# Row normalization on one core: a fixed transfer order on one queue, the last tile in halves, and a broadcast multiply

## The chip, the core and the metric

The kernel runs on one core of a Trainium2 chip. The metric is the device time of one execution in microseconds (us). Two engines compute here: VectorE (DVE in the profile, 190.8 us busy in the kernel before) and ScalarE (ACT, 56.7 us). SyncE (SP) issues the transfers between HBM and the on-chip memory (22 of them in the kernel before); the profile counts 16 DMA engines that carry them out.

In this text L3 is the load of tile 3 and S3 the store of tile 3; S7a and S7b are its first and second part where it is cut.

## The reference

```python
# x: float32 (32, 512, 1024)
sums = np.sum(np.abs(x), axis=-1, keepdims=True)
return (x / (sums + 1e-8)).astype(np.float32)
```

Each row of 1024 numbers is divided by the sum of its absolute values. 67.11 MB go in and 67.11 MB come out.

## The kernel before

The 16384 rows are cut into 8 tiles of 128 partitions x 16 rows. One tile is 8.39 MB; each partition's part of it is 64 KB, contiguous in HBM. Three tile buffers rotate.

```python
x_t = x_flat.rearrange("(n p r) d -> n p r d", p=P, r=R)       # R = 16
def process_chunk(x_tile, out_ap, r0, rN, mv):
    # ... cut: s = sum |x| per row, inv = 1 / s, both on VectorE; row = x_tile[:, r0 + r, :]
    for r in range(rN):
        if r < mv:
            nc.vector.tensor_scalar_mul(out=row, in0=row, scalar1=inv[:, r : r + 1])
        else:
            nc.scalar.activation(out=row, in_=row, func=Copy, scale=inv[:, r : r + 1])
    nc.sync.dma_start(out=out_ap[:, r0 : r0 + rN, :], in_=x_tile[:, r0 : r0 + rN, :])

for i in range(ntiles):
    nc.sync.dma_start(out=x_tile[:, :, :], in_=x_t[i, :, :, :])
    if i < ntiles - 2:
        process_chunk(x_tile, out_t[i], 0, R, 10)      # 10 rows on VectorE, 6 on ScalarE
    else:                                              # the last two tiles in quarters
        for c0 in range(0, R, 4):
            process_chunk(x_tile, out_t[i], c0, 4, 2)
```

The scheduler is free to order the instructions. On SyncE it made groups: L0-L2, S0-S2, L3-L5, S3-S5, L6, L7, then the eight quarter stores of tiles 6 and 7.

## Time and profile before

| | before |
|---|---|
| time, median of 3 | 318.28 us |
| span of the profile | 316.9 us |
| VectorE / ScalarE busy | 190.8 us (60%) / 56.7 us (18%) |
| DMA queue busy, share of 16 engines | 98.6% |
| bytes moved | 134.22 MB |

These lines are from the page of the kernel before: the busy time, the row of the 40 slices for DMA (each digit is the busy share in tenths), the queue with packets, MB and share, and the three costliest groups (line, engine, operation, shapes, count, then busy us, mean ns of one, and idle time before them with what ended it).

```profile
DVE 190.8 (60%) x104; ACT 56.7 (18%) x53; POOL 0.2 (0%) x4
DMA  9999999999999999999999999999999999999797
q1 hardware_dynamic: 3168, 134.22, 98.6%
L37 DVE TENSOR_REDUCE s<-x_tile 128x4 f32<-128x4096 f32 (+1 forms) x14 | 138.3, 9891 | 111.2 <-DMA x_tile<-in_x_dram 111.2
L54 ACT ACTIVATE x_tile<-x_tile,inv 128x1024 f32<-128x1024 f32 x52 | 55.4, 1137 | 223.9 <-DVE inv L45 223.9
L48 DVE TENSOR_SCALAR x_tile<-x_tile,inv 128x1024 f32<-128x1024 f32 x76 | 51.4, 748 | 0.3
```

The queue is full nearly everywhere, while VectorE waits 111 us for loads. The kernel is bound by its transfers. The one place where the queue is not full is near the end. The next lines are stretches of the same trace: from:to, length, busy us of VectorE, ScalarE and GpSimd, clock, DMA share, GB/s. (A packet seems to be booked where it starts, so a stretch near a packet's 2.4 us can swing, even above 1 (1.23 from 314 to 315 us of this trace).)

```profile
288.00:292.00 4.00, 4.00 (x3) 2.19 (x2) 0.00 (x0) 1.00 1.00 430
292.00:296.00 4.00, 4.00 (x6) 1.85 (x2) 0.00 (x0) 1.00 0.77 328
296.00:300.00 4.00, 4.00 (x4) 2.41 (x3) 0.00 (x0) 1.00 0.93 393
300.00:302.00 2.00, 1.97 (x5) 0.75 (x1) 0.00 (x0) 1.00 0.81 344
```

And these are two lines of SyncE's timeline there (start us, length, issue): the first quarter store of tile 7, and the other three.

```profile
294.09 0.33 SPq L60 DMA_DIRECT2D out_dram<-x_tile  x1
299.87 3.93 SPq L60 DMA_DIRECT2D out_dram<-x_tile  x3
```

VectorE is fully busy in these stretches. It is late with the second quarter of tile 7, and the queue runs short for a moment: that store was issued at 299.87 us, only 0.6 us before the store ahead of it had landed (300.43 us), and it landed 5.8 us after it, where the next two took 4.9 us each.

### The profile page before, as it was taken

The numbers are of one execution on the slowest core, as the hardware profiler recorded it, in microseconds if no ns is written. First come the engines' busy times: TensorE is split into PE (matmuls) and PEld (weight loads), VectorE is DVE, ScalarE is ACT, GpSimd is POOL, SyncE is SP. The second block draws the span as 40 slices with busy tenths as digits, with TensorE's granted clock in tenths as the row PEclk, the third lists the DMA queues.
The fourth block names the chain that finished last, engine by engine and source line by source line (L and its number), as shares of the span: only waits on it lengthen the run. The fifth ranks groups of instructions, "written<-read, shape, count | busy, mean of one in ns | idle before, by whom it ended". The sixth has DMA issues, their size and how long they took to land.

```text
span 316.9 us, 261 instructions
## 1 busy us (share of the span) xinstructions
DVE 190.8 (60%) x104; ACT 56.7 (18%) x53; POOL 0.2 (0%) x4
## 2 busy tenths in 40 slices
DVE  0019999999990000039999999980000069999910
ACT  0010080080080000000160070080000002522520
POOL 0000000000000000000000000000000000000000
DMA  9999999999999999999999999999999999999797
GB/s 397 397 397 513 414 397 397 397 438 488 397 397 505 422 397 397 521 405 397 480 447 397 397 489 438 397 430 480 414 397 480 438 405 422 399 431 432 335 430 331
DMA packets 3170, 134.24 MB, mean 424 GB/s; under 512 B 352, under 2 KB 352, under 8 KB 352
## 3 DMA queue, kind: packets, MB, share of 16 engines
q1 hardware_dynamic: 3168, 134.22, 98.6%
q14 instruction: 2, 0.02, 0.0%
HBM read 67.11 MB, written 67.11 MB: 424 GB/s over the span
## 4 chain that ended last, share of the span: by engine, by line
DVE 57%; DMA 35%; issue 4%; ACT 0%; ACTq 0%; SPq 0%; DVEq 0%
DVE s L37 41%; DMA x_tile<-in_x_dram 35%; DVE x_tile L48 15%; DVE inv L45 1%; ACT x_tile L54 0%; ACTq L99 0%; SPq L60 0%; DVEq L45 0%; DVEq L48 0%
## 5 line engine op out<-in xcount | busy, mean ns | idle before, releaser
L37 DVE TENSOR_REDUCE s<-x_tile 128x4 f32<-128x4096 f32 (+1 forms) x14 | 138.3, 9891 | 111.2 <-DMA x_tile<-in_x_dram 111.2
L54 ACT ACTIVATE x_tile<-x_tile,inv 128x1024 f32<-128x1024 f32 x52 | 55.4, 1137 | 223.9 <-DVE inv L45 223.9
L48 DVE TENSOR_SCALAR x_tile<-x_tile,inv 128x1024 f32<-128x1024 f32 x76 | 51.4, 748 | 0.3
L54 ACT ACT_TABLE_LOAD x1 | 1.3, 1283 | 22.8 <-DMA x_tile<-in_x_dram 22.8
L45 DVE RECIPROCAL inv<-s 128x4 f32<-128x4 f32 (+1 forms) x14 | 2.6, 200 | 0.4
L88 POOL MEMSET const-bfloat16-1.0<- 128x1 bf16 x1 | 0.1, 101 | 0.0
L88 POOL MEMSET const-uint8-127<- 128x1 uint8 x1 | 0.1, 101 | 0.0
L88 POOL MEMSET const-float32-0.0<- 128x1 f32 x1 | 0.1, 98 | 0.2 <-issue 0.2
L88 POOL MEMSET const-float32-1.0<- 128x1 f32 x1 | 0.1, 98 | 0.0
## 6 DMA issues: line engine op xcount, KB each, us to landing
out_dram<-x_tile SPq DMA_DIRECT2D x8, 2048.0 KB, 9.9
x_tile<-in_x_dram SPq DMA_DIRECT2D x8, 51.0
out_dram<-x_tile SPq DMA_DIRECT2D x6, 29.5
```

What stands on the lines that cost most here:

```text
L37: nc.vector.tensor_reduce(out=s[:, :], in_=x_tile[:, r0 : r0 + rN, :], axis=mybir.AxisListType.X, op=mybir.AluOpType.add, apply_absolute_v ...
L45: nc.vector.reciprocal(out=inv[:, :], in_=s[:, :])
L48: nc.vector.tensor_scalar_mul(out=x_tile[:, r0 + r, :], in0=x_tile[:, r0 + r, :], scalar1=inv[:, r : r + 1],)
L54: nc.scalar.activation(out=x_tile[:, r0 + r, :], in_=x_tile[:, r0 + r, :], func=mybir.ActivationFunctionType.Copy, scale=inv[:, r : r + 1],)
L88: nc = _bacc.Bacc("TRN2", target_bir_lowering=False, num_devices=1)
```

## The change

Its intent: keep one hardware queue always supplied, in an order written by hand (L0 L1 L2 S0 S1 L3 S2 L4 S3 L5 S4 L6 L7 S5 S6 S7); cut only the last tile, in halves; and replace the row-by-row VectorE multiplies by one multiply per tile.

```diff
+        nc.vector.tensor_scalar_add(out=s[:, :k], in0=s[:, :k], scalar1=EPS)
         ... reciprocal, as before ...
-        for r in range(rN):
-            if r < mv:
-                nc.vector.tensor_scalar_mul(out=row, in0=row, scalar1=inv[:, r : r + 1])
-            else: nc.scalar.activation(...)
+        nc.vector.tensor_mul(                                   # kv = k // 2
+            out=x_tile[:, r0 : r0 + kv, :],
+            in0=x_tile[:, r0 : r0 + kv, :],
+            in1=inv[:, :kv].unsqueeze(2).to_broadcast([P, kv, d]),
+        )
+        for r in range(kv, k): nc.scalar.activation(...)
     ... cut ...
+    plan = [("L", i) for i in range(BUFS)]
+    for i in range(ntiles):
+        plan.append(("S", i))
+        nxt = i + BUFS - 1
+        if BUFS <= nxt < ntiles:
+            plan.append(("L", nxt))
+    last = max(k for k, p in enumerate(plan) if p[0] == "L")
+    plan[last - 1], plan[last] = plan[last], plan[last - 1]
+    with tc.manual_schedule():
+        for what, i in plan:                # load(i) also emits the tile's arithmetic
+            load(i) if what == "L" else store(i)
```

More of the change, by code (lines that the diff above doesn't have):

```diff
@@ L7 @@
 from concourse._compat import with_exitstack
+FP32 = mybir.dt.float32
+EPS = 1e-8
 @with_exitstack
@@ L26, with normalize @@
     ntiles = n // (P * R)
+    BUFS = 3
     x_t = x_flat.rearrange("(n p r) d -> n p r d", p=P, r=R)
     out_t = out_flat.rearrange("(n p r) d -> n p r d", p=P, r=R)
-    BUFS = 3
     sbuf = ctx.enter_context(tc.tile_pool(name="sbuf", bufs=BUFS))
-    stats = ctx.enter_context(tc.tile_pool(name="stats", bufs=BUFS))
-    def process_chunk(x_tile, out_ap, r0, rN, mv):
-        s = stats.tile([P, rN], mybir.dt.float32, tag="s")
+    stats = ctx.enter_context(tc.tile_pool(name="stats", bufs=4))
+    def normalize(x_tile, r0, k, kv):
+        s = stats.tile([P, R], FP32)
         nc.vector.tensor_reduce(
-            out=s[:, :],
-            in_=x_tile[:, r0 : r0 + rN, :],
+            out=s[:, :k],
+            in_=x_tile[:, r0 : r0 + k, :],
             axis=mybir.AxisListType.X,
@@ L43, in process_chunk @@
         )
-        inv = stats.tile([P, rN], mybir.dt.float32, tag="inv")
-        nc.vector.reciprocal(out=inv[:, :], in_=s[:, :])
-        for r in range(rN):
-            if r < mv:
-                nc.vector.tensor_scalar_mul(
-                    out=x_tile[:, r0 + r, :],
-                    in0=x_tile[:, r0 + r, :],
-                    scalar1=inv[:, r : r + 1],
-                )
-            else:
-                nc.scalar.activation(
-                    out=x_tile[:, r0 + r, :],
-                    in_=x_tile[:, r0 + r, :],
-                    func=mybir.ActivationFunctionType.Copy,
-                    scale=inv[:, r : r + 1],
-                )
@@ L60, in process_chunk @@
-        nc.sync.dma_start(out=out_ap[:, r0 : r0 + rN, :], in_=x_tile[:, r0 : r0 + rN, :])
-    MV = 10
-    for i in range(ntiles):
-        x_tile = sbuf.tile([P, R, d], x.dtype)
-        nc.sync.dma_start(out=x_tile[:, :, :], in_=x_t[i, :, :, :])
-        if i < ntiles - 2:
-            process_chunk(x_tile, out_t[i], 0, R, MV)
-        else:
-            C = 4
-            for c0 in range(0, R, C):
-                process_chunk(x_tile, out_t[i], c0, C, (MV * C) // R)
+        nc.vector.tensor_scalar_add(out=s[:, :k], in0=s[:, :k], scalar1=EPS)
@@ new lines, in normalize @@
+        inv = stats.tile([P, R], FP32)
+        nc.vector.reciprocal(out=inv[:, :k], in_=s[:, :k])
+        nc.vector.tensor_mul(
[3 more added lines that the diff above has]
+        )
+        for r in range(kv, k):
+            row = x_tile[:, r0 + r, :]
+            nc.scalar.activation(
+                out=row,
+                in_=row,
+                func=mybir.ActivationFunctionType.Copy,
+                scale=inv[:, r : r + 1],
+            )
@@ new lines, in span, with load, store @@
+    def span(i):
+        k = R // 2 if i == ntiles - 1 else R
+        return [(r0, k) for r0 in range(0, R, k)]
+    tiles = {}
+    def load(i):
+        x_tile = sbuf.tile([P, R, d], FP32)
+        tiles[i] = x_tile
+        for r0, k in span(i):
+            nc.sync.dma_start(
+                out=x_tile[:, r0 : r0 + k, :], in_=x_t[i][:, r0 : r0 + k, :]
+            )
+        for r0, k in span(i):
+            normalize(x_tile, r0, k, k // 2)
+    def store(i):
+        for r0, k in span(i):
+            nc.sync.dma_start(
+                out=out_t[i][:, r0 : r0 + k, :], in_=tiles[i][:, r0 : r0 + k, :]
+            )
@@ L77 @@
+    plan = [("L", i) for i in range(BUFS)]
[8 more added lines that the diff above has]
+        for what, i in plan:
+            if what == "L":
+                load(i)
+            else:
+                store(i)
 _INS = ['x']
```

## The prediction

> **What bounds the kernel now.** The page's busy table has VectorE at 60% and ScalarE at 18% of the 316.9 us span; the DMA row shows nine tenths in all slices but two near the end, and the one hardware queue holds 98.6% of the 16 engines' span. From the landings in the trace, one 8.39 MB transfer, load or store, follows the last every 19.2 to 19.5 us, about 434 GB/s. [...] Sixteen transfers at 19.35 us are 309.6 us. What is left, some 7 us, is all that a better order can win:
> - 3.4 us at the start (first load lands at 22.8 us);
> - 1.1 us at the third load (a gap of 20.5 us), no cause visible;
> - about 1 us in the last tile: its second quarter-store was issued only at 299.87 us, 5.8 us after the first (timeline of SyncE), and landed 5.76 us after it where others need 4.87; the DMA share falls to 0.77 and 0.81 in stretches there;
> - about 1 us after the last landing.
>
> The chain of waits names VectorE for 57%, but it walks back through a queue that never empties: while VectorE idles 44 us for a load, the DMA is full.
>
> **What the change does.**
> - Scaling: ten rows at 748 ns on VectorE (6.7 us a tile) and six at 1134 ns on ScalarE become one two-tensor multiply of 8 rows beside 8 ScalarE rows. [...] the trace has no such instruction yet. ScalarE: 8.5 us. The reduce stays at 17.2 us, a small add of 0.2 us comes in. A tile costs VectorE 26.4 us instead of 24.2; DMA needs 38.7 us per tile (load and store). Off the critical path.
> - Order: stores and loads alternate (S1 L3 S2 L4 ... L6 L7 S5 S6 S7) instead of three by three. Working it through, the queue never empties: tightest is store 1, issued at about 75.5 us, when store 0 runs until 82; later the slack is 15 us or more. So the order moves no end time: the queue was full before.
> - Tail: after the last load, at about 256 us, three tiles' stores remain (58 us of transfers), and the last half is ready at about 290 us, long before its turn. The 1 us of starvation goes.
>
> **Prediction.** 22.8 + 15 x 19.35 + 1 to 2 us gives a profiled span of 314 to 315.5 us; with the 1.4 us between span and time before: 316.7 us, range 315.4 to 318.4. Chances: faster by over 2% 0.01, within 2% 0.96, slower 0.03. Faster needs under 311.9 us, only 2.3 us for start and end together.
>
> **What would show it.** DMA slices at nine tenths to the end, no dip near 295 us; a multiply of about 8.7 us; VectorE busy about 210 us, ScalarE about 70; landings still 19.35 us apart.
>
> **What would make it wrong.** If ScalarE waits for the broadcast multiply, the first store slips past 57 us and store 1 to about 84: an idle DMA of 2 to 3 us. A multiply at half the expected rate does much the same, once, at the start. If alternating reads and writes changed the rate of a transfer by 1%, the time would move 3 us; the trace shows loads and stores equally fast, but hardly mixed.

Two passages are cut from the prediction, at the marks. 22.8 + 15 x 19.35 + 1 to 2 us comes to 314.05 to 315.05 us, put as 314 to 315.5, and the 1.4 us lead to 316.7. VectorE's 26.4 us a tile is 17.2 us for the reduce, 0.2 for the add, about 0.25 for the reciprocal, and the remaining 8.7 for the multiply. The trace of the changed kernel has 26.36 us from the first reduce to the second (22.55 to 48.91 us), 8.69 of them in the multiply. The times that build on this part (store 1 issued at 75.5 us, the last half ready at 290, VectorE busy about 210) were measured as 75.4, 292.9 and 211.0 us. That a transfer takes no less than the measured 19.2 us was the assumption; the shortest step of 8.39 MB in the two traces is 19.21 us.

## The result, and the profile after

The median was 317.57 us (317.45 to 319.79, 6 runs), beside 318.26 us for the kernel before. The ratio is 0.9997, with a 95% interval of 0.9975 to 1.0019. Ratios here are the mean time of one kernel's fast runs over that of the other's in the same rounds, so they are not quite the ratio of the medians. All runs of both count as fast. Four runs of the changed kernel lay between 317.45 and 317.58 us and two at 319.38 and 319.79; the kernel before stayed within 0.6 us (within 1.0 us in every later set). The changed kernel has gained nothing on the mean, and it has become less steady. The profiled execution was the one of 319.38 us.

These lines of the page of the changed kernel answer to those of before.

```profile
DVE 211.0 (66%) x36; ACT 68.8 (22%) x65; POOL 0.2 (0%) x4
DMA  9999999999999999999999999999999999999994
q1 hardware_dynamic: 2592, 134.22, 98.3%
L40 DVE TENSOR_REDUCE s<-x_tile 128x16 f32<-128x16384 f32 (+1 forms) x9 | 137.9, 15320 | 80.7 <-DMA x_tile<-in_x_dram 80.7
L57 ACT ACTIVATE x_tile<-x_tile,inv 128x1024 f32<-128x1024 f32 x64 | 67.5, 1136 | 201.3 <-DVE inv L49 191.9
L50 DVE TENSOR_TENSOR x_tile<-x_tile,inv 128x8192 f32<-128x8192 f32 (+1 forms) x9 | 69.7, 7744 | 0.6
```

VectorE works 20 us more and waits 30 us less; the queue has no dip before its end. By these lines the plan worked. The last microseconds tell another story. These are stretches of the changed kernel's trace, in the same columns:

```profile
310.00:313.00 3.00, 0.00 (x0) 0.00 (x0) 0.00 (x0) 1.00 0.94 404
313.00:314.00 1.00, 0.00 (x0) 0.00 (x0) 0.00 (x0) 1.00 0.16 66
314.00:315.00 1.00, 0.00 (x0) 0.00 (x0) 0.00 (x0) 1.00 0.00 0
315.00:316.00 1.00, 0.00 (x0) 0.00 (x0) 0.00 (x0) 1.00 0.08 33
```

From 313 us on hardly a packet starts, and by the packet records 15 of the 16 engines are done at 314.2 us. 33 GB/s over the microsecond from 315 us is 33 KB, which is one packet of 32 KB: a single engine starts its last packet when the others have finished.

**How to see one engine in a trace that adds up sixteen.** In the traces of both kernels every transfer leaves 16 increments of its semaphore, and they come apart: for the last half-store of the changed kernel 15 come from 313.40 to 314.60 us and one at 316.68. The packet records show the same split: the last packets of 15 engines end by 314.22 us, and that of one at 316.31. So I read each increment as one engine that has done its part. By this reading the median of the 16 times tells when a typical engine is done, the last one when the transfer has landed; I call the difference the lag. This table is worked out from those increments: for each transfer the landing minus the previous landing, and the lag, in us.

| | L1 | L2 | S0 | S1 | L3 | S2 | L4 | S3 | L5 | S4 | L6 | L7 | S5 | S6 | S7 |
|---|---|---|---|---|---|---|---|---|---|---|---|---|---|---|---|
| changed kernel, step | 19.33 | 20.50 | 19.41 | 19.66 | 19.89 | 19.42 | 20.62 | 19.31 | 19.95 | 19.37 | 19.34 | 19.40 | 19.37 | 19.30 | 19.30 |
| changed kernel, lag | 0.25 | 0.34 | 0.41 | 0.20 | 1.08 | 0.82 | 2.41 | 2.09 | 2.84 | 2.59 | 2.88 | 2.86 | 2.90 | 2.89 | 2.90 |

Most of the time is lost in L2, L3, L4 and L5, and these are loads with a store behind them in the queue. (A store in front of a load, as S1, comes some tenths late on the median engine too, which makes the lag of L3 and its like look larger beside it; the median makes that good with the next load, 19.87 us for S1 and 19.00 for L3.) The DMA records, one for each packet, say where within them. A packet of 64 KB took 2418 ns on the median. By following the packets from engine to engine, the packets more than 150 ns above that were, apart from the 16 first ones of L0: the last of the 8 packets of L2 on all 16 engines, the last of L3 on 11, of L4 on 7, of L5 on 11, and only four others, three of them on the engine that ends last. That engine took 3805, 3033 and 3541 ns for its last packets of L2, L3 and L4.

In the kernel before, stores follow loads in the queue at three places only (L2-S0, L5-S3, L7-S6), in the changed kernel at five (L2-S0, L3-S2, L4-S3, L5-S4, L7-S5). The kernel before also had a lag, 1.20 us at the last quarter store of tile 6. But then its queue ran short: the first quarter of tile 7 landed with a lag of 0.17 us. The engines that were ahead had waited for VectorE, and the late one had caught up meanwhile. So of the 1.9 us that the median engine lost there (the two first quarter stores of tile 7 took 5.87 and 5.83 us, where the last two took 4.88), the last engine lost only 0.9.

### The profile page after: what moved, and what is told of

It is laid out like the page before. It is cut to its first block, busy times and chain, and to the rows that moved or that the text cites. A ratio compares the mean times of both kernels' runs of the same rounds, so it can differ in the third digit from the quotient of the medians.

```text
span 317.6 us, 193 instructions
## 1 busy us (share of the span) xinstructions
DVE 211.0 (66%) x36; ACT 68.8 (22%) x65; POOL 0.2 (0%) x4
## 3 DMA queue, kind: packets, MB, share of 16 engines
q1 hardware_dynamic: 2592, 134.22, 98.3%
## 4 chain that ended last, share of the span: by engine, by line
DVE 50%; DMA 30%; another core or an unknown queue 12%; issue 0%; DVEq 0%; SPq 0%
DVE s L40 33%; DMA x_tile<-in_x_dram 19%; DVE x_tile L50 16%; DMA out_dram<-x_tile 10%; DVE inv L49 1%; DVE s L47 0%; DVEq L50 0%; SPq L82 0%
## 5 line engine op out<-in xcount | busy, mean ns | idle before, releaser
L40 DVE TENSOR_REDUCE s<-x_tile 128x16 f32<-128x16384 f32 (+1 forms) x9 | 137.9, 15320 | 80.7 <-DMA x_tile<-in_x_dram 80.7
L57 ACT ACTIVATE x_tile<-x_tile,inv 128x1024 f32<-128x1024 f32 x64 | 67.5, 1136 | 201.3 <-DVE inv L49 191.9
L50 DVE TENSOR_TENSOR x_tile<-x_tile,inv 128x8192 f32<-128x8192 f32 (+1 forms) x9 | 69.7, 7744 | 0.6
L49 DVE RECIPROCAL inv<-s 128x16 f32<-128x16 f32 (+1 forms) x9 | 2.2, 242 | 0.3
L47 DVE TENSOR_SCALAR s<-s 128x16 f32<-128x16 f32 (+1 forms) x9 | 1.6, 174 | 0.3
```

What stands on the lines that cost most here:

```text
L40: nc.vector.tensor_reduce(out=s[:, :k], in_=x_tile[:, r0 : r0 + k, :], axis=mybir.AxisListType.X, op=mybir.AluOpType.add, apply_absolute_v ...
L47: nc.vector.tensor_scalar_add(out=s[:, :k], in0=s[:, :k], scalar1=EPS)
L49: nc.vector.reciprocal(out=inv[:, :k], in_=s[:, :k])
L50: nc.vector.tensor_mul(out=x_tile[:, r0 : r0 + kv, :], in0=x_tile[:, r0 : r0 + kv, :], in1=inv[:, :kv].unsqueeze(2).to_broadcast([P, kv, d]),)
L57: nc.scalar.activation(out=row, in_=row, func=mybir.ActivationFunctionType.Copy, scale=inv[:, r : r + 1],)
```

## The experiments

A switch, below, is a place in the queue where a store follows a load. **Theory 1:** each switch of the queue from a load to a store holds up one or another of the 16 engines at the load's last packet; the lags add up, and the slowest engine sets the end. The shortage that the change removed had cost the slowest engine only 0.9 us, and the added switches cost about as much. **Theory 2:** the lag comes at random, whatever the order. A further question was what the two parts of the change do alone.

Unless said otherwise each experiment ran next to the kernel before on the same chip, in the same rounds. The chips of different sets differ by some tenths of a microsecond (medians of the kernel before: 318.52, 318.67, 318.64 and 318.47 us on chips 0, 15, 2 and 12). The edits below are shortened.

### The changed kernel again (three repeats)

No edit.

> The changed kernel, unaltered, to see how often its time falls near 317.5 us and how often near 319.5 us (4 and 2 of 6 so far). Theory 1 (each switch of the queue from a load to a store holds up one or another of the 16 DMA engines, and the slowest engine sets the end): two clusters or a spread again, each profile with a last engine that lost its time at the ends of L2, L3, L4 or L5 and nowhere else. Theory 2 (a lag that comes at random, in any kernel): the lag of the last engine, 2.88 us in the first profile, grows also in the middle of runs of like transfers.

> The changed kernel, unaltered, on the chip of the other three: 317.4 to 320.1 us, spread over 2 us, mean near 318.4.

> The changed kernel, unaltered, on the same chip as the two others: 317.4 to 320.5 us, mean near 318.5.

Measured: medians of 318.62 (317.59 to 320.14, 6 runs), 318.35 (318.06 to 320.49, 6) and 317.98 us (317.63 to 318.71, 5); ratios to the kernel before 1.0006, 1.0004 and 0.9987. The times do not fall in two clean clusters, as the first six had suggested, but spread over 3 us. Over all four sets 23 runs have a mean of 318.45 us, and 39 runs of the kernel before in the same sets 318.49 us. Each set has one profile, and the time of each profiled execution follows from its landings:

| profiled execution | time | first load landed to last store landed | of this, lag at the end |
|---|---|---|---|
| first | 319.38 | 294.16 | 2.90 |
| second | 319.36 | 294.07 | 2.26 |
| third | 318.80 | 293.54 | 1.66 |
| fourth | 317.63 | 292.25 | 0.67 |

The time is the middle column plus 25.2 to 25.4 us each time. The spread of the changed kernel is the spread of its slowest engine. In the first and the third profile the lag grew mainly in L3, L4 and L5. In the second and third it also grew, by 0.8 and 0.3 us, in L7b, which is again a load before a store. The second shows a further rise, of 0.5 us, in L6, which no store follows, and less than half of its rise comes in L3 to L5 (about 1 of 2.1 us); so switches are not the only source.

### Fewer switches, first try

```diff
-    plan = ...   # 5 switches from load to store
+    order = "L0 L1 L2 S0 S1 S2 L3 L4 L5 S3 S4 L6 L7 S5 S6 S7"   # 3 switches
+    plan = [(p[0], int(p[1:])) for p in order.split()]
```

> The changed kernel with its transfers put in groups (L0-2, S0-2, L3-5, S3-4, L6-7, S5-7): 3 switches from load to store instead of 5, everything else the same, no starving queue. Theory 1: all times together at 316.8 to 317.6 us, no cluster at 319.5, lag of the last engine in the profile below 1.5 us. Theory 2: the same two clusters as the changed kernel.

Measured: 321.06 us (320.88 to 321.42, 5 runs), ratio 1.0081. Neither theory had said so, and the fault was in the experiment. S2 landed 22.69 us after S1 instead of 19.3. These stretches of its trace show the gap (a packet's booking shifts it by up to 2.4 us):

```profile
96.00:100.00 4.00, 4.00 (x1) 4.00 (x5) 0.00 (x0) 1.00 0.61 262
100.00:104.00 4.00, 1.71 (x1) 1.44 (x2) 0.00 (x0) 1.00 0.63 262
104.00:108.00 4.00, 0.00 (x0) 0.00 (x0) 0.00 (x0) 1.00 1.21 524
```

And this line of SyncE's timeline (start us, length, issues) shows that three stores were issued between 49.09 and 102.11 us, the last of them S2:

```profile
49.09 53.02 SPq L82 DMA_DIRECT2D out_dram<-x_tile  x3
```

With the new arithmetic tile 2 is ready only at 101.7 us. In this order nothing stands between S1 and S2, so the queue runs dry; in the order of the change L3 stands between them. The lag at the end was only 0.49 us, as theory 1 has it, but one test with a fault proves little, so it is repeated below. One step of this run does not fit a small cost of later switches: L5, the load before the second switch, took 20.54 us instead of about 19.35, after the queue had run dry.

### Many switches against few, with half tiles

Both kernels use tiles of 8 rows (4.19 MB a transfer, packets of 32 KB) and 6 buffers: the same memory, bytes, packets and instructions. Only the order differs.

```diff
-    R = 16 ; BUFS = 3
+    R = 8 ; BUFS = 6
     # ... cut: more small buffers; no tile is cut in halves (both kernels)
     # few: groups of 6, 6 and 4 loads, each followed by its stores    (3 switches)
+    for g in (range(0, 6), range(6, 12), range(12, 16)):
+        plan += [("L", i) for i in g] + [("S", i) for i in g]
     # many: L0 L1 L2 S0 L3 S1 L4 S2 ... L15 S13 S14 S15               (14 switches)
```

> Control for the next run: tiles of 8 rows (4.19 MB a transfer, 6 buffers, the same memory), in groups of 6, 6 and 4 loads and stores: 3 switches from load to store. Theory 1: as the grouped kernel, 316.8 to 317.8 us. Theory 2: as the changed kernel, about 317.5 and 319.5.

> Tiles of 8 rows, loads and stores strictly alternating after three loads: 14 switches from load to store, the same bytes, packets and instructions as the control. Theory 1: the median engine loses some 0.1 us a switch (0.23, 0.07 and 0.19 us in the first profile of the changed kernel) and the last engine more: 319.5 to 325 us. Theory 2: within 0.5 us of the control. The stall of about 1.15 us that all engines show at the end of the third load should move to about 30 us, before the first store, if it belongs to the first store; if it belongs to the clock it stays near 59 us.

Measured: 317.29 us (317.19 to 317.32, 5 runs) with 3 switches and 321.81 us (321.15 to 322.27, 4 runs) with 14; ratios to the kernel before 0.9960 (0.9948 to 0.9973) and 1.0101 (1.0088 to 1.0115). The DMA row of the slices with 3 switches:

```profile
DMA  8999999999999999999999999999999999999996
```

The same row with 14 switches:

```profile
DMA  8999999999999999999999999999999999999994
```

Both queues are full to the last slice; nothing in these rows explains 4.5 us. The landings do: the lag at the end is 0.94 us with 3 switches and 4.27 us with 14, and the median engine ends 1.20 us later (314.98 and 313.78 us). These two parts, 3.3 and 1.2 us, make up the 4.5 us between the last landings. Theory 2 falls as the explanation of the whole. A remainder of it stands: of the 0.94 us that are left with 3 switches, 0.4 came in the last load but one, which no store follows.

The stall that all engines show in the last load before the first store moved with that store. With the first store behind the third half-load, that load took 10.76 us (10.58 on the median engine) instead of 9.7, at about 33 us on the span's clock; with the first store behind the sixth, the sixth took 10.36 us, at about 62 us. It belongs to the first switch, not to the clock. The kernel before has it too, so it was no loss that this change could have removed.

Theory 1 is not shown as it stands either, because not each switch costs something. With 3 switches, the loads before the second and third, L11 and L15, took 9.72 and 9.71 us, as any other load, and only two packets there were over 150 ns longer than the median. With 14 switches, such packets stood at the end of every load before a store but the last, on 2 to 16 engines. The two orders differ in two things: the number of switches, and that from L3 on each load of the second order stands alone, with a store in front of it as well as behind. The experiments change both together, so they do not tell which of the two counts.

### Fewer switches, second try

The order of the change with the old arithmetic (10 rows one by one on VectorE, 6 on ScalarE; in the halves 5 and 3; no add), and then the same kernel in groups.

```diff
-    nc.vector.tensor_mul(... broadcast ...)          # both kernels
+    for r in range(k): tensor_scalar_mul if r < 10 * k // 16 else activation
-    plan = ...                                       # second kernel only
+    order = "L0 L1 L2 S0 S1 S2 L3 L4 L5 S3 S4 L6 L7 S5 S6 S7"
```

> The change's transfer order and halves with the old arithmetic (10 rows one by one on VectorE, 6 on ScalarE; 5 and 3 in the halves; no add). If only the order of transfers sets the end: the same spread as the changed kernel, 317.4 to 320 us. If the broadcast multiply had a part in the lag of the engines, it should be tighter than that, near 317.3 us.

> The order-only kernel (old arithmetic, last tile in halves) with its transfers in groups: 3 switches from load to store instead of 5. The old 24.2 us a tile let the third store be issued at about 95.5 us, before the queue runs dry at 101. Theory 1 (switches): 317.2 to 317.9 us, lag of the last engine at the end below 1.5 us; the order-only kernel took 319.5 us with a lag of 2.77 us. If the number of switches does not matter with packets of 64 KB: 319 to 320 us.

Measured: 319.53 us (318.54 to 320.07, 6 runs, ratio 1.0023, interval 1.0008 to 1.0038) with five switches and 317.58 us (316.89 to 318.61, 6 runs, ratio 0.9973, interval 0.9959 to 0.9988) with three. They ran in different sets, so it is the two ratios that compare: half a per cent apart, and the intervals don't meet. The lag at the end was 2.77 and 0.42 us in the two profiles. Once the arithmetic is in time, fewer switches win with packets of 64 KB too. That the old arithmetic has the lag as well clears the broadcast multiply of it. It did not come out tight, however: with three switches the times still spread over 1.7 us, and the profiled execution, of 316.89 us, was the fastest of the six, so its lag is not the typical one.

### The arithmetic alone

```diff
-        for r in range(rN): tensor_scalar_mul for r < mv, activation for the rest   # MV = 10
+        tensor_scalar_add; reciprocal; one broadcast tensor_mul of mv rows; activation # MV = 8
```

The transfers stay as in the kernel before.

> The kernel before with the change's arithmetic alone (small add, broadcast multiply of 8 of 16 rows, 2 of 4 in the quarters, ScalarE the rest), transfers in the old order. If VectorE's work is hidden wherever the queue is full, as the prediction held, the time stays at 318.5 us. If the old order hides only the old 24.2 us a tile: the store of the third tile is issued at about 101.7 us instead of 95.5, after the queue has run dry at about 101, which costs some 3.3 us as in the grouped kernel, and the quarter chunks at the end get about 1 us longer each: 322 to 325 us.

Measured: 331.65 us (331.49 to 331.80, 4 runs), ratio 1.0405. So the direction was that of the second reading, and the size was larger than its 322 to 325 us. The landings show four late stores: S2 came 22.56 us after S1, S5 22.70 us after S4, S7a 9.15 us after S6d, and S7b 6.70 us after that. Beside the same steps of the kernel before (19.47, 19.51, 4.85 and 5.76 us) these are 3.1, 3.2 and, for the last two together, 5.2 us more: 11.5 of the 13.0 us by which the medians differ. L5 and L7, the loads before the later switches, add 1.2 and 0.7 us (20.56 and 20.29 us, instead of 19.39 and 19.56), and the other steps give 0.4 us back. So the same switch L5-S3, in the same order of transfers, cost nothing to speak of in the kernel before and 1.2 us here, after the queue had run dry. I had forgotten S5, which stands in the second group as S2 does in the first, and I had underestimated the tail. These lines of its trace give the reason for the late stores: the multiply of a tile took 8692 ns, that of a quarter 2288 ns in place of two rows of 748 ns.

```profile
L47 DVE TENSOR_TENSOR x_tile<-x_tile,inv 128x8192 f32<-128x8192 f32 x6 | 52.2, 8692 | 0.2
L47 DVE TENSOR_TENSOR x_tile<-x_tile,inv 128x2048 f32<-128x2048 f32 x8 | 18.1, 2288 | 0.1
```

The new arithmetic costs 4% in the old order and nothing in the new one, where a load always stands between two stores until the last load. The prediction's "off the critical path" is true of the two parts together only.

### The shortage at the end alone

```diff
-                process_chunk(x_tile, out_t[i], c0, C, (MV * C) // R)   # 2 of 4 rows on VectorE
+                process_chunk(x_tile, out_t[i], c0, C, 1)               # 1 of 4
```

> The kernel before with 1 row of 4 on VectorE in the quarter chunks instead of 2, so that VectorE is done some 4 us earlier and the queue should no longer run dry before the second quarter of the last tile. The queue before lost 1.97 us there on the median engine, but only 0.9 us on the last one. Expected: a gain of 0.9 us or a little less (317.5 to 317.8 us), with the lag of the last engine at the end back at about 1.2 us instead of 0.1. If the lag did not matter, the gain would be 2 us (316.5 us).

Measured: 317.62 us (317.38 to 318.96, 6 runs), ratio 0.9971 (0.9955 to 0.9987). All the quarter stores of tile 7 now landed 4.85 to 4.87 us apart, and the lag at the end was 0.82 us instead of 0.10. The shortage was worth 0.9 us, not 2: the last engine had used part of it to catch up. This is the prize that the change was out for, and one number in the old kernel collects it.

### The size of the packets

Same order, same transfers, but the 16 rows of a partition are taken from HBM in two blocks of 8, four of 4, or 16 single rows.

```diff
-    x_t = x_flat.rearrange("(n p r) d -> n p r d", p=P, r=R)                       # 64 KB packets
+    x_t = x_flat.rearrange("(n a p b) d -> n p a b d", p=P, b=8, a=2)              # 32 KB; b=4, a=4: 16 KB
+    x_t = x_flat.rearrange("(n r p) d -> n p r d", p=P, r=R)                       # 4 KB
```

> The changed kernel with row r of a tile in partition p taken from row 128r+p, so that every packet is 4 KB instead of 64 KB (another shape of the same traffic, same order, 5 switches from load to store). In the profiles so far a switch holds up the last packet of the load. If the loss goes with the size of that packet, the lag of the last engine falls below 0.5 us and the time to about 316.5 us, tight; if a switch costs what it costs, 317.4 to 320 us as before; if packets of 4 KB are slower by themselves, the steps between landings rise above 19.35 us and the time goes up in proportion.

> The changed kernel with each partition's 16 rows of a tile in two blocks of 8: packets of 32 KB instead of 64 KB, transfers of the same size in the same order. If what a switch costs goes with the size of the packet: lag of the last engine at the end about 1.2 to 1.6 us (64 KB: 2.3 to 2.9; 4 KB: 0.5), time 317 to 318 us. If it goes with the size of the transfer or the number of switches only: lag 2.3 to 2.9 us, 317.5 to 320 us.

> The same with four blocks of 4 rows, packets of 16 KB. If the cost goes with the packet: lag about 0.6 to 0.9 us at the end, but a transfer takes about 19.5 us instead of 19.35 (the quarter stores of the kernel before, of such packets, followed each other in 4.87 us): 317 to 318.5 us, tight.

| packets | time, median (range) | ratio | step, plain load | last load before the first store (median engine) | lag at the end |
|---|---|---|---|---|---|
| 64 KB (four profiles above) | 317.57 to 318.62 | 0.9987 to 1.0006 | 19.33 | 20.4 | 0.67 to 2.90 |
| 32 KB | 318.74 (317.85 to 319.48) | 1.0006 | 19.42 | 20.24 | 1.41 |
| 16 KB | 318.51 (318.37 to 319.02) | 1.0000 | 19.57 | 19.98 | 0.59 |
| 4 KB | 328.90 (328.86 to 329.22) | 1.0321 | 20.47 | 20.47 | 0.50 |

The stall at the first switch shrinks with the packet, from 1.1 us (20.4 minus 19.33) over 0.8 and 0.4 to nothing, so what it costs goes with the size of the packet (the order of the HBM addresses within a transfer changes along with it, which these runs do not separate). For the lag the trend is the same, but the 64 KB kernel alone ranges from 0.67 to 2.90 us, so one profile of each proves little. The times did not come down as the packet reading expected for 32 KB (317 to 318 us). Smaller packets do not help in the end: each transfer gets longer by about as much. With 4 KB a load takes 20.47 us and a store 19.8 to 19.9, 5.9% and about 3% more than with 64 KB (19.33 and 19.3).

### Stores on a queue of their own

```diff
     def store(i):
-            nc.sync.dma_start(
+            nc.scalar.dma_start(
-    plan = ...
+    plan = [(what, i) for i in range(ntiles) for what in ("L", "S")]
```

> The changed kernel with its stores issued by ScalarE on a queue of its own, each right after its tile is scaled, and loads on the old queue as soon as a buffer is free. If the loss belongs to a load and a store that follow each other in one queue, it goes away: 316.5 to 317.3 us. If reading and writing at once costs by itself, the engines now mix packets of both for most of the time, and the time rises above the changed kernel's: 320 us or more.

Measured: 325.22 us (323.23 to 329.98, 6 runs), ratio 1.0186 (1.0157 to 1.0214) by its four fast runs, a verdict of unclear. The profiled execution, of 328.17 us, counts as slow, and no fast one (323.23 to 326.42 us) has a trace. It looks like the second expectation, but in this trace the loss has another place. Stretches of it:

```profile
160.00:260.00 100.00, 69.88 (x9) 16.86 (x16) 0.00 (x0) 1.00 1.01 434
260.00:285.00 25.00, 22.63 (x8) 12.69 (x12) 0.00 (x0) 1.00 1.02 439
285.00:300.00 15.00, 4.53 (x1) 0.00 (x0) 0.00 (x0) 1.00 0.52 227
```

While both queues have work, mixed packets move at 434 and 439 GB/s. The same stretches have 430 and 446 GB/s in the fourth profile of the changed kernel, with one queue. So the mix of reads and writes was not slower by itself here, and the second queue brought no second bandwidth. What is lost in this execution is the order: S6, issued at 269.39 us, ran beside the last half-load, whose reduce started only at 295.47 us, and the queues stood empty while VectorE worked on it (DMA share 0.00 from 298 to 304 us). Whether the lag at the switches goes away with two queues can't be read from this run, and whether the faster executions lost their time in the same place is not shown.

### The better version again

The half-tile kernel with three switches, unaltered, in another set.

> The half-tile kernel with 3 switches again, as the candidate that beats both: 317.2 to 317.4 us, all within 0.3 us, some 1.2 us below the kernel before.

Measured: 317.51 us (317.31 to 318.22, 5 runs), ratio 0.9969 (0.9957 to 0.9981). One of five runs lay outside the 0.3 us that I had expected. In both sets it beats the kernel before by 0.3 to 0.4%, and the changed kernel ran in both sets at the kernel before's mean. It has the new arithmetic and the old number of switches, and pieces small enough that no store comes too late.

## Why the prediction was wrong, point by point

- **What bounds the kernel: right.** Both kernels are bound by the transfers (98.6% and 98.3% of the 16 engines' span; a plain load or store of 8.39 MB every 19.3 us, 434 GB/s); no kernel came below 316.89 us.
- **The costs of the arithmetic: right in size.** The multiply, forecast at about 8.7 us (on a basis that no trace showed then), was measured as 8692 ns, 1.06 ns an element of a partition, where the row multiplies of before took 748 ns for 1024, or 0.73. VectorE was busy for 211.0 us (about 210 predicted), ScalarE 68.8 (about 70). The slack worked out for S1 was there: it was issued at about 75.4 us, before the queue ran out.
- **"Off the critical path": right only with the new order.** Alone the arithmetic cost 4%.
- **"The 1 us of starvation goes": right.** Alone it was worth 0.9 us.
- **"So the order moves no end time": wrong.** This is the step that failed. I treated the 16 engines as one that delivers a transfer every 19.35 us. The new order has five switches from load to store instead of three, three of them at loads that stand alone between stores, and single engines fell behind there. The lag at the end was 0.67 to 2.90 us in four profiles, where the kernel before ended with 0.10. With the arithmetic of before, the new order was 0.23% slower than the kernel before, and the grouped order 0.27% faster.
- **The mis-sized term** stands in "22.8 + 15 x 19.35 + 1 to 2 us". Its 1 to 2 us were used up by the stall at the first switch (1.1 us) and by the 0.9 us after the last landing. Nothing was left for the lag. From the first landing to the last, 15 x 19.35 is 290.25 us; the four profiles had 292.25 to 294.16.
- **A smaller error of the same sum:** I added 1.4 us between span and time, from a profile and a median of different executions. Within one execution it is about 1.8 us.
- **"If alternating reads and writes changed the rate":** the last sentence came near. The rate did not change, as 434 GB/s in a constant mix show, but the ends of single packets did, at each change-over.
- I forecast a gain of 1.6 us. The medians of the first set differ by 0.7 us and the means of four sets by 0.04 us. The first median, 317.57 us, lies inside the range that I gave, but that is no success of the reasoning: the range was wide enough to hold the kernel before's own 318.26 us.

What stays open: why the last packet of a load can take longer when a store follows it, whether the number of switches or the loads that stand alone between stores make the loss, why the same switch L5-S3 cost 0.04 us in one run and 1.2 us in another, why one engine can be hit far more than the others, and where the smaller rises with no switch behind them come from (0.3 to 0.7 us: L6 in the kernel before and in one profile of the changed one, the last load but one in both profiles of the half tiles). The runs show when it happens and that it shrinks with the packet, not its mechanism.

## What to carry to other kernels

A queue that is full by its average can still end late, because a transfer has landed only with the last of its engines (here the queue was busy for 98.3%, and the last engine was done 2.90 us after the median one): look at the sixteen increments of a transfer, not only at the busy share. In a kernel bound by transfers, try loads and stores in groups as large as the buffers allow: in the two pairs tested here they beat alternation by 0.5% and 1.4%. But check at each place where two stores follow each other that the second one's data is ready (S2 landed 22.69 and 22.56 us after S1 in two runs where it was not, instead of 19.3 to 19.5). A short idle moment may be hiding another delay, so removing it can return less than its length (here 0.9 of 1.9 us).
